# A hybrid encoder layer on one core: order of copies and differences, banks of the latent projections, first x block

## Chip, core and metric

The kernel runs on one core of one Trainium2 chip. The metric is the device time of one execution in microseconds (us); the median of three runs before the change is 1478.06 us (1475.95 to 1479.08). TensorE is called PE here, VectorE DVE, ScalarE ACT, GpSimd POOL, and SyncE's DMA queue SP, as in the profile.

## The reference

One encoder layer on 256 tokens of width 2048, all in float32. A projection of the normalised input feeds two groups of eight heads; the stretch that matters below lies where the first group ends and the second begins:

```python
h = rmsnorm(x, ln_mix); proj = h @ w_in
q_na, k_na, v_na, c_q, c_kv, k_rope = split(proj)          # widths 1024 x3, 512, 256, 64
y_na  = neighbourhood_attention(q_na, k_na, v_na, na_rpb)  # 8 heads of 128, softmax with bias
q  = rmsnorm(c_q, q_norm) @ w_uq      # 8 heads: 128 latent + 64 rotary columns
kv = rmsnorm(c_kv, kv_norm) @ w_ukv   # 8 heads: 128 keys + 128 values
y_mla = softmax((q_nope k_nope^T + rope(q_rope) rope(k_rope)^T) * s) v
x = x + concat(rmsnorm(y_na), rmsnorm(y_mla)) @ w_out
x = x + memory_attention(rmsnorm(x), rmsnorm(mem))         # 4 heads, 256 memory tokens
x = x + swiglu(rmsnorm(x));  return rmsnorm(x)
```

## The kernel before

**Two parts of every operand.** Each float32 operand is split into a high part (ACT copies it into the format fp32r) and a low part (DVE subtracts the high part from the source). `split` (L107) issues one copy and one difference. A product is three matmuls: high by high, high by low, low by high (`products`, L220; `products_fm`, L202, with the weights as the stationary side).

**Weights** come as 496 pieces of 128x1024, two to a DMA on SP, through three raw buffers. `Weights.piece` (L158) keeps up to two pieces split ahead of the one in use (one ahead for the first 16), so every piece costs ACT one copy (`whi`, L110) and DVE one difference (`wlo`, L111), in the same queues as all other work. The first piece is split in two halves, and between them `first_x` splits the first two blocks of x (`xs`, L113 and L114).

**PSUM** has two pools. `psm` (L70) has two buffers of two banks for the long accumulations `pm`; `psa` (L71) has four buffers of one bank for everything short: `pt` (a turn, that is four transposes, L295), `ps` (scores), `py` (a head's output), `pv`, `pc`. A buffer is free when its last reader is done.

**Order.** The main program issues the long products in a written order. Side work (turns, scores, softmax, splits of results) sits in generators in `Background` (L167), advanced by `bg.tick()` after each block of products, so that short work lies between long products. Each engine runs its own instructions strictly in the order issued; an instruction whose wait isn't over holds up all behind it.

**The latent stretch** (L605 to L618): `project_v(0)`, `project_k(0)`, `project_v(1)`, `project_k(2)`, the rotary part of q, `project_q(0)`, `project_q(1)`, then the output projection, with `project_q(2)` and `(3)` inside it. Results go to `ml` (values in the first half, keys in the second), `qn` and `rt`. `project_k` (L573) and `linear_fm` (L208, used by `project_q`) take a `psm` buffer per pair of heads, each of its two tiles of 128x256 in a bank of its own. `split_v` (L343) splits a `psm` buffer in two parts, one per half of the tokens. Beside it, the last head of the first group (`s`, `pk`, `py`, `vy_na`, and `sq`, the square of its output) and the normalised q latent (`ct`, turned into `cs` by `turn_job`, L303) are finished.

Of the kernel before, what the change touches and what calls it, by code (L numbers as in the profile page):

```python
# [60 lines left out]
def tile_hybrid_encoder(ctx, tc, x, xt, mem, memt, gains, fgain, rope, rpb, weights, out):  # L61
# [21 lines left out]

    def load_x(j, queue):
        xf[j] = scr.tile([P, 2, T], F32, name="xf", tag=("ev", "gate")[j % 2])
        queue.dma_start(xf[j], x[:, 2 * j:2 * j + 2, :])

    load_x(0, nc.scalar)

# [14 lines left out]
    ready = const.tile([P, TT], F32, name="ready")  # L104
    nc.scalar.activation(ready, neghalf, AF.Copy)

    def split(dst_hi, dst_lo, src, scale=None):  # L107

        if scale is None:
            ordered(nc.scalar.activation(dst_hi, src, AF.Copy))  # L110
            ordered(nc.vector.tensor_sub(dst_lo, src, dst_hi.bitcast(F32)))  # L111
        else:
            ordered(nc.scalar.activation(dst_hi, src, AF.Copy, scale=scale))  # L113
            ordered(nc.vector.scalar_tensor_tensor(dst_lo, src, scale, dst_hi.bitcast(F32),  # L114
                                           op0=OP.mult, op1=OP.subtract))

    class Weights:

# [14 lines left out]
        def split(self):  # L133
            p = self.done
            self.done += 1
            r, j = divmod(p, 2)
            cuts = (0, PE_EL // 2, PE_EL) if p == 0 else (0, PE_EL)
            cuts = [slice(j * PE_EL + a, j * PE_EL + b) for a, b in zip(cuts, cuts[1:])]
            self.load(r + (1 if p < 2 else 1 + j if p < EARLY else RAWS))
            raw = self.raw[r]  # L140
            if p < 2:
                for c in cuts:
                    nc.sync.dma_start(raw[:, c], weights[r, :, c])
                    if c.start == 0:
                        nc.sync.dma_start(gain, gains)
            if p >= N_PIECE - HELD:
                hi, lo = (self.held[:, p - N_PIECE + HELD, i] for i in range(2))
            else:
                hi = wp.tile([P, PE_EL], F32R, name="whi", tag="whi", bufs=SPLITS)
                lo = wp.tile([P, PE_EL], F32R, name="wlo", tag="wlo", bufs=SPLITS)  # L150
            for c in cuts:
                if c.start and p == 0:
                    self.first_x()
                d = slice(c.start - j * PE_EL, c.stop - j * PE_EL)
                split(hi[:, d], lo[:, d], raw[:, c])
            self.parts[p] = hi, lo

        def piece(self):  # L158
# [60 lines left out]

    def products(o, ak, t, hi, lo, first, last):  # L220

# [81 lines left out]
    def turn_job(src, f0, nf, dst, g0=None, wait=2):  # L303

        for f in range(0, nf, 2):
            pt = turn(src, f0 + f)
            if g0 is None:
                d = dst(f, 2)
                split(d[:, :, 0, :], d[:, :, 1, :], pt)
# [32 lines left out]

    def split_v(pm, dst, rc=None):  # L343

        for t in range(TT):
            v = (pm[t] if isinstance(pm, list) else pm[:, t, :]).rearrange("p (h d) -> p h d", d=P)
            ts_ = slice(t * P, (t + 1) * P)
            split(dst[:, :, 0, ts_], dst[:, :, 1, ts_], v, None if rc is None else rc[:, t:t + 1])


    def softmax_steps(s, scale, pkp, done):

        nm = scr.tile([P, TT], F32, name="nm", tag="nm", bufs=4)
# [19 lines left out]
        split(pk[:, :, 0, :], pk[:, :, 1, :], pt)  # L373
        done(pk)

    def mm_values(py, v, pk):
# [10 lines left out]
    with ExitStack() as at:  # L387
# [17 lines left out]
        def split_x(j):  # L405
            for i in range(2):
                k = 2 * j + i
                split(xs[:, k, 0, :], xs[:, k, 1, :], xf[j][:, i, :], gain[:, G_MIX + k:G_MIX + k + 1])

        wt.first_x = lambda: split_x(0)  # L410
        n_x = KB // 2
        for j in range(n_x):
            ks = range(2 * j, 2 * j + 2)
# [49 lines left out]
        def compressed(pm, w, name, b0, nb_):  # L463
# [17 lines left out]
            if name == "kv":  # L481
                kr = scr.tile([P, TT, 2, ROPE], F32, name="kr", tag="kr")
                for t in range(TT):
                    rotate(kr[:, t, 0:1], kt[:, t:t + 1, :], t, 1)
                    nc.gpsimd.tensor_copy(kr[:, t, 1], kr[:, t, 0])
                yield W_TR
                pt = turn(kr.rearrange("p t j c -> p t (j c)"), 0, 1)
                for i in range(2):
                    rows = slice(i * ROPE, (i + 1) * ROPE)
                    split(krs[i][rows, 0, :], krs[i][rows, 1, :], pt[rows, 0, :])  # L490

        bg.add(compressed(linear(xs, KB, cw=KVR), RANK_KV, "kv", 4, 2))

# [5 lines left out]
        def head_out(vy, h, acc, g0, pk):  # L499

            assert done[g0] == h
            done[g0] += 1
            py = psa.tile([P, T], F32, name="py", tag="a")
            mm_values(py, vy[:, h], pk)
            split(vy[:, h, 0, :], vy[:, h, 1, :], py, gain[:, g0 + h:g0 + h + 1])
            square_into(acc, py[:, None, :], h == 0)

        def na_head(h, qt, wait):
            yield wait
            pt = turn(qt, 2 * (h % 2))  # L510
            qk = nap.tile([P, 2, 2, T], F32R, name="qk", tag="qk", bufs=2)
            split(qk[:, :, 0, :], qk[:, :, 1, :], pt)
            yield W_QK
            ps = psa.tile([P, TT, T], F32, name="ps", tag="a")
            for t in range(TT):
# [10 lines left out]
        def rope_job(pm):  # L526
# [5 lines left out]
            for f in range(0, 4, 2):  # L532
                pt = turn(rt, f)
                qr = ap.tile([P, 2, 2, T], F32R, name="qr", tag="qr", bufs=2)
                split(qr[:, :, 0, :], qr[:, :, 1, :], pt)
                qrs[f], qrs[f + 1] = qr[:, 0], qr[:, 1]
                yield 2

# [21 lines left out]
        def q_job(pair, pm):  # L560
            yield 1
            qn = mlp().tile([P, 2, 2, T], F32R, name="qn", tag="qn", bufs=4)
            split(qn[:, :, 0, :], qn[:, :, 1, :], pm)
            qns[pair] = qn

        def k_job(pair, pm):
            yield 1
            kn = kns[:, 2 * pair:2 * pair + 2]
            split(kn[:, :, 0, :], kn[:, :, 1, :], pm)

        def project_q(pair):
            bg.add(q_job(pair, linear_fm(cs, 4)))
# [1 line left out]
        def project_k(pair):  # L574
            hi, lo = wt.piece()
            for i in range(2):
                pm = psm.tile([P, 2, 2 * T], F32, name="pm", tag="pm")
                for k in range(2):
                    for f in range(2):
                        s = slice(k * 512 + i * 256 + f * P, k * 512 + i * 256 + (f + 1) * P)  # L580
                        products_fm(pm[:, f, 0:T], hi[:, s], lo[:, s], cs[:, 4 + k], k == 0, k == 1)
                    bg.tick()
                bg.add(k_job(pair + i, pm[:, :, 0:T]))

        def project_v(i):
            split_v(linear(cs[:, 4:6], 2), vy_ml[:, 4 * i:4 * i + 4])
# [45 lines left out]
    with ExitStack() as at:  # L632
# [5 lines left out]
        def load_mem():  # L638
            for i in range(4):
# [2 lines left out]
                yield 8  # L642
                for j in range(0, 4, 2):
                    yield 8
                    for k in range(4 * i + j, 4 * i + j + 2):
                        split(ms[:, k, 0, :], ms[:, k, 1, :], r[:, k - 4 * i, :], gain[:, G_MEM + k:G_MEM + k + 1])
# [38 lines left out]
        def xv_job(h, pm):  # L685
# [3 lines left out]
            for j in range(4):  # L689
                py = psa.tile([P, T], F32, name="py", tag="a")  # L690
                mm_values(py, vn[:, j], pks[h])
                o = block(os_, 4 * h + j)
                split(o[:, 0, :], o[:, 1, :], py)
                yield 2

        for h in range(XH):
# [171 lines left out]
```

## Time and profile before

| | us |
|---|---|
| median of three runs (lowest, highest) | 1478.06 (1475.95, 1479.08) |
| the profiled execution's own time | 1475.9 |
| its span, first to last instruction | 1474.0 |
| PE busy in the span | 1452.6 |
| DVE busy | 806.5 |
| ACT busy | 701.4 |
| mean granted TensorE clock | 0.997 |

The span and the profiled execution's own time differ by 1.9 us of start and end. Matmuls are pipelined: a row of PE has the time from its start to its modelled end, and the next one starts before that end. So a gap between two matmuls costs the distance of their starts less the usual distance, which is more than the idle time that a row shows.

### The profile page before, as it was taken

To read this page: it belongs to the slowest core of one execution; us is meant where nothing else is said; L and a number is where in the kernel's file an instruction comes from. 1 tells how busy PE (TensorE), PEld (TensorE's weight loads), DVE (VectorE), ACT (ScalarE), POOL (GpSimd) and SP (SyncE) were. 2 spreads that over 40 slices of the span, in tenths; PEclk is the share of its full clock that TensorE was granted. 3 is DMA by queue.
4 is the path that set the end of the run, shared out by engine and by line. 5 is a ranking of instruction groups with operands and counts; after the bars stand their busy time and mean duration, and the time that the engine had idled before them with its cause. 6 is when DMAs were issued, how large, how long until landed. Compare 5 with 4: busy or idle time off the path is not lost.

```text
span 1474.0 us, 17024 instructions
## 1 busy us (share of the span) xinstructions
PE 1452.6 (99%) x6860; PEld 1214.0 (82%) x6860; DVE 806.5 (55%) x908; ACT 701.4 (48%) x934; POOL 22.1 (2%) x39
## 2 busy tenths in 40 slices
PE   9999989999999999999999999999999999999997
PEld 7888878888888888888888888888888888888886
DVE  5576667666545555555555555455454445555554
ACT  5656554456555454445454444444343444444443
POOL 0000000000000000000000000000000000000000
PEclk9999999999999999999999999999999999999999
DMA  9794443355665444545555555555555555555553
GB/s 345 243 246 159 153 142 127 131 212 173 232 232 179 146 169 149 179 162 197 175 196 186 185 198 187 187 197 178 196 200 192 186 194 192 183 197 187 185 199 114
DMA packets 48717, 275.89 MB, mean 187 GB/s; under 512 B 12992, under 2 KB 13120, under 8 KB 16576
## 3 DMA queue, kind: packets, MB, share of 16 engines
q1 hardware_dynamic: 48208, 273.51, 54.6%
q10 hardware_dynamic: 432, 1.31, 0.3%
q8 instruction: 53, 0.87, 0.2%
q14 instruction: 24, 0.20, 0.0%
HBM read 272.71 MB, written 3.05 MB: 187 GB/s over the span
## 4 chain that ended last, share of the span: by engine, by line
PE 95%; DVE 2%; ACT 1%; DMA 1%; issue 1%; POOL 0%; SPq 0%; POOLq 0%; ACTq 0%
PE pm L223 28%; PE pm L225 28%; PE pm L224 28%; PE pt L300 2%; PE ps L195 2%; PE py L195 2%; PE pv L224 1%; PE pv L225 1%; PE pv L223 1%; DVE wlo L111 1%; DMA raw<-in_weights 1%; PE pl L225 0%; PE pl L223 0%; PE pl L224 0%; ACT whi L110 0%
## 5 line engine op out<-in xcount | busy, mean ns | idle before, releaser
L111 DVE TENSOR_TENSOR wlo<-raw,whi 128x1024 fp32r<-128x1024 f32 (+1 forms) x493 | 601.9, 1222 | 539.5 <-ACT whi L110 538.9
L110 ACT ACTIVATE whi<-raw 128x1024 fp32r<-128x1024 f32 (+1 forms) x493 | 520.5, 1058 | 534.6 <-PE pm L225 502.9
L223 PE MATMUL pm<-whi,x3s 128*128 128x512 f32 x704 | 275.8, 392 | 0.0
L225 PE MATMUL pm<-whi,x3s 128*128 128x512 f32 x704 | 274.1, 389 | 0.0
L224 PE MATMUL pm<-wlo,x3s 128*128 128x512 f32 x704 | 273.9, 389 | 0.0
L225 PEld LDWEIGHTS pm<-whi,x3s 128*128 128x128 f32 x704 | 132.1, 188 | 27.7
L224 PEld LDWEIGHTS pm<-wlo,x3s 128*128 128x128 f32 x704 | 132.2, 188 | 26.8
L223 PEld LDWEIGHTS pm<-whi,x3s 128*128 128x128 f32 x704 | 132.2, 188 | 26.8
L223 PE MATMUL pm<-whi,ms 128*128 128x512 f32 x256 | 101.7, 397 | 0.0
L224 PE MATMUL pm<-wlo,ms 128*128 128x512 f32 x256 | 99.9, 390 | 0.0
L225 PE MATMUL pm<-whi,ms 128*128 128x512 f32 x256 | 99.8, 390 | 0.0
L223 PE MATMUL pm<-whi,ha 128*128 128x512 f32 x224 | 87.5, 391 | 0.0
L225 PE MATMUL pm<-whi,ha 128*128 128x512 f32 x224 | 87.2, 389 | 0.0
L224 PE MATMUL pm<-wlo,ha 128*128 128x512 f32 x224 | 87.1, 389 | 0.0
L223 PE MATMUL pm<-whi,xs 128*128 128x512 f32 (+1 forms) x192 | 74.2, 387 | 0.2 <-ACT whi L110 0.2
L224 PE MATMUL pm<-wlo,xs 128*128 128x512 f32 (+1 forms) x192 | 72.4, 377 | 0.8 <-DVE wlo L111 0.8
L225 PE MATMUL pm<-whi,xs 128*128 128x512 f32 (+1 forms) x192 | 72.5, 378 | 0.0
L225 PEld LDWEIGHTS pm<-whi,ms 128*128 128x128 f32 x256 | 48.1, 188 | 10.4
L223 PEld LDWEIGHTS pm<-whi,ms 128*128 128x128 f32 x256 | 48.2, 188 | 8.9
L224 PEld LDWEIGHTS pm<-wlo,ms 128*128 128x128 f32 x256 | 48.2, 188 | 8.7
L223 PE MATMUL pm<-whi,x2s 128*128 128x512 f32 x128 | 50.0, 391 | 0.0
L225 PE MATMUL pm<-whi,x2s 128*128 128x512 f32 x128 | 49.8, 389 | 0.0
(240 smaller groups left out, 1918.3 us busy)
## 6 DMA issues: line engine op xcount, KB each, us to landing
raw<-in_weights SPq DMA_DIRECT2D x247, 1024.0 KB, 5.0
xr<-in_xt SPq DMA_DIRECT2D x2, 1024.0 KB, 11.2
bias<-skew SPq DMA_DIRECT2D x16, 128.0 KB, 8.3
mtok<-in_memt SPq DMA_DIRECT2D x4, 512.0 KB, 5.1
mraw<-in_mem SPq DMA_DIRECT2D x4, 512.0 KB, 5.6
xf<-in_x SPq DMA_DIRECT2D x7, 256.0 KB, 8.4
fg<-in_fgain SPq DMA_DIRECT2D x1, 1024.0 KB, 9.6
out<-xr SPq DMA_DIRECT2D x2, 512.0 KB, 3.8
```

Of the source, the lines that this page charges most:

```text
L110: ordered(nc.scalar.activation(dst_hi, src, AF.Copy))
L111: ordered(nc.vector.tensor_sub(dst_lo, src, dst_hi.bitcast(F32)))
L195: ordered(nc.tensor.matmul(ps, a[:, u, :], b[:, v, :], start=first and i == 0, stop=last and i == 2))
L223: ordered(nc.tensor.matmul(o, ak[:, 0, ts_], hi, start=first, stop=False))
L224: ordered(nc.tensor.matmul(o, ak[:, 0, ts_], lo, start=False, stop=False))
L225: ordered(nc.tensor.matmul(o, ak[:, 1, ts_], hi, start=False, stop=last))
L300: ordered(nc.tensor.transpose(pt[:, f, t * P:(t + 1) * P], src[:, t, (f0 + f) * P:(f0 + f + 1) * P], ident))
```

## The change

Three edits.

1. `split` takes several parts and issues all copies, then all differences. Callers that had a loop over two parts (`split_v`, `turn_job` with a gain, the blocks of x, the memory's blocks) now pass both at once.
2. `linear_fm` and `project_k` take one bank of `psa` per pair of heads (tile `pf`) in place of a `psm` buffer. Both 256-column tiles lie in that bank; the loop over them is now outside the loop over the contraction, so that one tile is finished before the next begins. The ticks stand at the same distances.
3. The first block of x comes in two DMAs of one half each, both issued on ACT's queue. `first_x` splits the first half between the halves of the first weight piece and the second half after it.

```diff
     def load_x(j, queue):
         xf[j] = scr.tile([P, 2, T], F32, name="xf", tag=("ev", "gate")[j % 2])
-        queue.dma_start(xf[j], x[:, 2 * j:2 * j + 2, :])
+        for i in range(2) if j == 0 else (slice(0, 2),):
+            queue.dma_start(xf[j][:, i], x[:, 2 * j:2 * j + 2, :][:, i])
...
-    def split(dst_hi, dst_lo, src, scale=None):
-
-        if scale is None:
-            ordered(nc.scalar.activation(dst_hi, src, AF.Copy))
-            ordered(nc.vector.tensor_sub(dst_lo, src, dst_hi.bitcast(F32)))
+    def split(*parts):
+
+        for hi, lo, src, scale in parts:
+            if scale is None:
+                ordered(nc.scalar.activation(hi, src, AF.Copy))
...
+        for hi, lo, src, scale in parts:
+            if scale is None:
+                ordered(nc.vector.tensor_sub(lo, src, hi.bitcast(F32)))
...
                 if c.start and p == 0:
-                    self.first_x()
+                    self.first_x((0,))
...
+            if p == 0:
+                self.first_x((1,))
...
-        pm = psm.tile([P, 2, 2 * T], F32, name="pm", tag="pm")
-        for k in range(nk):
-            if k % 4 == 0:
-                hi, lo = wt.piece()
-            for f in range(2):
+        pm = psa.tile([P, 2, T], F32, name="pf", tag="a")
+        assert nk == 4
+        hi, lo = wt.piece()
+        for f in range(2):
+            for k in range(nk):
                 s = slice(k % 4 * T + f * P, k % 4 * T + (f + 1) * P)
-                products_fm(pm[:, f, 0:T], hi[:, s], lo[:, s], block(a, k), k == 0, k == nk - 1)
-            bg.tick()
-        return pm[:, :, 0:T]
+                products_fm(pm[:, f, :], hi[:, s], lo[:, s], block(a, k), k == 0, k == nk - 1)
+                if k % 2:
+                    bg.tick()
+        return pm
...
             else:
-                for j in range(2):
-                    d = dst(f + j, 1)
-                    split(d[:, 0, 0, :], d[:, 0, 1, :], pt[:, j, :], gain[:, g0 + f + j:g0 + f + j + 1])
+                d = dst(f, 2)
+                split(*((d[:, j, 0, :], d[:, j, 1, :], pt[:, j, :], gain[:, g0 + f + j:g0 + f + j + 1])
+                        for j in range(2)))
...
+        parts = []
         for t in range(TT):
...
-            split(dst[:, :, 0, ts_], dst[:, :, 1, ts_], v, None if rc is None else rc[:, t:t + 1])
+            parts.append((dst[:, :, 0, ts_], dst[:, :, 1, ts_], v, None if rc is None else rc[:, t:t + 1]))
+        split(*parts)
...
-                pm = psm.tile([P, 2, 2 * T], F32, name="pm", tag="pm")
-                for k in range(2):
-                    for f in range(2):
+                pm = psa.tile([P, 2, T], F32, name="pf", tag="a")
+                for f in range(2):
+                    for k in range(2):
```

What the built programs show: the instructions of each engine stand in the same order as before (but for the loops' inner order and the first x block); what differs is what they wait for. In brackets are the engines or DMA semaphores that a row waits for.

PE, second tile of keys and the last head's output behind it, before: the tile's first matmul waits for a buffer of `psm`.

```order
L204 MATMUL pm<-cs,whi 128x256 [waits DVE_49,PE_49]
L205 MATMUL pm<-cs,whi 128x256
L206 MATMUL pm<-cs,wlo 128x256
...
L195 MATMUL py<-pk,vy_na 128x256 [waits Activation_49]
L195 MATMUL py<-pk,vy_na 128x256 x5
L223 MATMUL pm<-whi,cs 128x512 [waits DVE_49]
```

The same place on PE after the change, down to the turn of the q latent.

```order
L211 MATMUL pf<-cs,whi 128x256 [waits PE_49]
L212 MATMUL pf<-cs,whi 128x256
L213 MATMUL pf<-cs,wlo 128x256
...
L202 MATMUL py<-pk,vy_na 128x256 [waits Activation_49]
L202 MATMUL py<-pk,vy_na 128x256 [waits DVE_49]
L202 MATMUL py<-pk,vy_na 128x256 x4
L231 MATMUL pm<-whi,cs 128x512
...
L308 MATMUL pt<-ident,ct 128x128 [waits DVE_49,PE_49]
L308 MATMUL pt<-ident,ct 128x128 [waits DVE_49]
```

The keys and the values behind them no longer wait for DVE; the turn does, for `ct`, which it did not have to name before.

ACT, the two copies of the first values (`ml` from `pm`, 4x128) and of the first turned q latent (`cs`), before.

```order
L110 ACTIVATE ml<-pm 128x4x128 [waits PE_49]
L110 ACTIVATE ml<-pm 128x4x128 [waits DVE_49]
L110 ACTIVATE whi<-raw 128x1024
L110 ACTIVATE ml<-pm 128x2x256 [waits PE_49]
...
L113 ACTIVATE cs<-pt,gain 128x256 [waits PE_49]
L113 ACTIVATE cs<-pt,gain 128x256 [waits DVE_49]
```

The same place on ACT after the change.

```order
L112 ACTIVATE ml<-pm 128x4x128 [waits PE_49]
L112 ACTIVATE ml<-pm 128x4x128
L112 ACTIVATE whi<-raw 128x1024
L112 ACTIVATE ml<-pf 128x2x256 [waits PE_49]
...
L114 ACTIVATE cs<-pt,gain 128x256 [waits PE_49]
L114 ACTIVATE cs<-pt,gain 128x256
```

The second copy of a pair waits for nothing of its own; before, it waited for the first difference.

## Rows read from the trace of the kernel before

**Rows 1.** The page, busy us of each engine (share of the span), instructions.

```profile
PE 1452.6 (99%) x6860; PEld 1214.0 (82%) x6860; DVE 806.5 (55%) x908; ACT 701.4 (48%) x934; POOL 22.1 (2%) x39
```

**Rows 2.** Waits of PE, whole span: engine line, releaser, total us, times, longest.

```profile
PE pv L223 <- ACT xs L113: 1.3, 1, 1.3
```

**Rows 3.** Timeline of PE, 200 to 256 us: start, us, what, [idle before, releaser].

```profile
203.95 0.35 PE L204 MATMUL pm<-cs,whi 128*128 128x256 f32 x1 [2.90 <-DVE ml L111]
...
204.26 0.28 PE L206 MATMUL pm<-cs,wlo 128*128 128x256 f32 x1
204.38 0.28 PE L204 MATMUL pm<-cs,whi 128*128 128x256 f32 x1
...
206.73 0.50 PE L223 MATMUL pm<-whi,cs 128*128 128x512 f32 x1 [0.40 <-DVE ml L111]
...
208.22 0.60 PE L300 MATMUL pt<-ident,ct 128*128 128x128 f32 x4
208.58 0.48 PE L223 MATMUL pm<-whi,cs 128*128 128x512 f32 x1
...
212.24 0.36 PE L204 MATMUL pm<-cs,whi 128*128 128x256 f32 x1 [2.02 <-DVE ml L111]
...
217.70 0.50 PE L223 MATMUL pm<-whi,cs 128*128 128x512 f32 x1 [0.38 <-DVE ml L111]
...
226.97 0.35 PE L204 MATMUL pm<-cs,whi 128*128 128x256 f32 x1 [0.66 <-DVE rotb L460]
...
230.56 0.47 PE L223 MATMUL pm<-whi,vy_na 128*128 128x512 f32 x1 [0.49 <-DVE qn L111]
...
255.95 0.47 PE L223 MATMUL pm<-whi,vy_na 128*128 128x512 f32 x1 [1.10 <-DVE qn L111]
```

**Rows 4.** Windows: stretch, its us, busy us of each engine, granted clock, DMA.

```profile
199.47:234.21 34.74, 27.89 (x167) 24.47 (x166) 25.22 (x37) 17.53 (x27) 1.44 (x2) 0.95 0.42 146
212.00:217.00 5.00, 4.76 (x27) 4.79 (x28) 3.54 (x7) 2.98 (x5) 0.00 (x0) 0.66 0.15 21
```

**Rows 5.** Timeline of ACT in the latent stretch.

```profile
200.30 0.60 ACT L110 ACTIVATE ml<-pm 128x512 fp32r<-128x512 f32 x1
202.49 0.60 ACT L110 ACTIVATE ml<-pm 128x512 fp32r<-128x512 f32 x1 [1.59 <-DVE ml L111]
...
207.39 0.38 ACT L255 ACTIVATE sq<-py 128x256 f32<-128x256 f32 x1 [0.55 <-DVE vy_na L114]
207.68 1.05 ACT L110 ACTIVATE whi<-raw 128x1024 fp32r<-128x1024 f32 x1
...
210.41 0.47 ACT L113 ACTIVATE cs<-pt,gain 128x256 fp32r<-128x256 f32 x1 [1.07 <-DVE cs L114]
```

**Rows 6.** Timeline of DVE in the latent stretch.

```profile
201.77 0.68 DVE L111 TENSOR_TENSOR ml<-pm,ml 128x512 fp32r<-128x512 f32 x1
203.12 0.69 DVE L111 TENSOR_TENSOR ml<-pm,ml 128x512 fp32r<-128x512 f32 x1 [0.66 <-ACT ml L110]
204.06 1.23 DVE L111 TENSOR_TENSOR wlo<-raw,whi 128x1024 fp32r<-128x1024 f32 x1 [0.25 <-ACT whi L110]
205.20 0.88 DVE L478 TENSOR_SCALAR ct<-ct,rc_q 128x512 f32<-128x512 f32 x2
205.99 0.68 DVE L111 TENSOR_TENSOR ml<-pm,ml 128x512 fp32r<-128x512 f32 x1
...
209.90 0.48 DVE L114 SCALAR_TENSOR_TENSOR cs<-pt,gain,cs 128x256 fp32r<-128x256 f32 x1
```

**Rows 7.** The chain that ended last, 0 to 16 us: start, us, what.

```profile
3.06 8.47 DMA raw<-in_weights
...
13.93 0.50 PE pv L224
...
14.67 0.23 PE pv L223
```

**Rows 8.** Timeline of SP's queue, 0 to 11 us.

```profile
5.77 0.33 SPq L86 DMA_DIRECT2D xf<-in_x  x1
```

More of the change, by code (lines that the diff above doesn't have):

```diff
@@ L152, in split @@
                 if c.start and p == 0:
-                    self.first_x()
+                    self.first_x((0,))
                 d = slice(c.start - j * PE_EL, c.stop - j * PE_EL)
-                split(hi[:, d], lo[:, d], raw[:, c])
+                split((hi[:, d], lo[:, d], raw[:, c], None))
+            if p == 0:
+                self.first_x((1,))
             self.parts[p] = hi, lo
@@ L308, in turn_job @@
                 d = dst(f, 2)
-                split(d[:, :, 0, :], d[:, :, 1, :], pt)
+                split((d[:, :, 0, :], d[:, :, 1, :], pt, None))
             else:
-                for j in range(2):
-                    d = dst(f + j, 1)
-                    split(d[:, 0, 0, :], d[:, 0, 1, :], pt[:, j, :], gain[:, g0 + f + j:g0 + f + j + 1])
+                d = dst(f, 2)
+                split(*((d[:, j, 0, :], d[:, j, 1, :], pt[:, j, :], gain[:, g0 + f + j:g0 + f + j + 1])
+                        for j in range(2)))
             if f + 2 < nf:
@@ L372, in softmax_steps @@
         pk = pkp.tile([P, TT, 2, T], F32R, name="pk", tag="pk")
-        split(pk[:, :, 0, :], pk[:, :, 1, :], pt)
+        split((pk[:, :, 0, :], pk[:, :, 1, :], pt, None))
         done(pk)
@@ L403, in tile_hybrid_encoder, with split_x @@
         px = parts_tile("x")
[L405 to L410, printed above, removed]
+        def split_x(j, blocks=range(2)):
+            split(*((xs[:, 2 * j + i, 0, :], xs[:, 2 * j + i, 1, :], xf[j][:, i, :],
+                     gain[:, G_MIX + 2 * j + i:G_MIX + 2 * j + i + 1]) for i in blocks))
+        wt.first_x = lambda blocks: split_x(0, blocks)
         n_x = KB // 2
@@ L489, in compressed @@
                     rows = slice(i * ROPE, (i + 1) * ROPE)
-                    split(krs[i][rows, 0, :], krs[i][rows, 1, :], pt[rows, 0, :])
+                    split((krs[i][rows, 0, :], krs[i][rows, 1, :], pt[rows, 0, :], None))
         bg.add(compressed(linear(xs, KB, cw=KVR), RANK_KV, "kv", 4, 2))
@@ L504, in head_out @@
             mm_values(py, vy[:, h], pk)
-            split(vy[:, h, 0, :], vy[:, h, 1, :], py, gain[:, g0 + h:g0 + h + 1])
+            split((vy[:, h, 0, :], vy[:, h, 1, :], py, gain[:, g0 + h:g0 + h + 1]))
             square_into(acc, py[:, None, :], h == 0)
@@ L511, in na_head @@
             qk = nap.tile([P, 2, 2, T], F32R, name="qk", tag="qk", bufs=2)
-            split(qk[:, :, 0, :], qk[:, :, 1, :], pt)
+            split((qk[:, :, 0, :], qk[:, :, 1, :], pt, None))
             yield W_QK
@@ L534, in rope_job @@
                 qr = ap.tile([P, 2, 2, T], F32R, name="qr", tag="qr", bufs=2)
-                split(qr[:, :, 0, :], qr[:, :, 1, :], pt)
+                split((qr[:, :, 0, :], qr[:, :, 1, :], pt, None))
                 qrs[f], qrs[f + 1] = qr[:, 0], qr[:, 1]
@@ L562, in q_job @@
             qn = mlp().tile([P, 2, 2, T], F32R, name="qn", tag="qn", bufs=4)
-            split(qn[:, :, 0, :], qn[:, :, 1, :], pm)
+            split((qn[:, :, 0, :], qn[:, :, 1, :], pm, None))
             qns[pair] = qn
@@ L568, in k_job @@
             kn = kns[:, 2 * pair:2 * pair + 2]
-            split(kn[:, :, 0, :], kn[:, :, 1, :], pm)
+            split((kn[:, :, 0, :], kn[:, :, 1, :], pm, None))
         def project_q(pair):
@@ L576, in project_k @@
             for i in range(2):
-                pm = psm.tile([P, 2, 2 * T], F32, name="pm", tag="pm")
-                for k in range(2):
-                    for f in range(2):
+                pm = psa.tile([P, 2, T], F32, name="pf", tag="a")
+                for f in range(2):
+                    for k in range(2):
                         s = slice(k * 512 + i * 256 + f * P, k * 512 + i * 256 + (f + 1) * P)
-                        products_fm(pm[:, f, 0:T], hi[:, s], lo[:, s], cs[:, 4 + k], k == 0, k == 1)
+                        products_fm(pm[:, f, :], hi[:, s], lo[:, s], cs[:, 4 + k], k == 0, k == 1)
                     bg.tick()
-                bg.add(k_job(pair + i, pm[:, :, 0:T]))
+                bg.add(k_job(pair + i, pm))
         def project_v(i):
@@ L644, in load_mem @@
                     yield 8
-                    for k in range(4 * i + j, 4 * i + j + 2):
-                        split(ms[:, k, 0, :], ms[:, k, 1, :], r[:, k - 4 * i, :], gain[:, G_MEM + k:G_MEM + k + 1])
+                    split(*((ms[:, k, 0, :], ms[:, k, 1, :], r[:, k - 4 * i, :], gain[:, G_MEM + k:G_MEM + k + 1])
+                            for k in range(4 * i + j, 4 * i + j + 2)))
             for g in range(DM // CW):
@@ L692, in xv_job @@
                 o = block(os_, 4 * h + j)
-                split(o[:, 0, :], o[:, 1, :], py)
+                split((o[:, 0, :], o[:, 1, :], py, None))
                 yield 2
```

9 lines of the change are left out of this document (5 added, 4 removed).

## The prediction

> **What bounds the kernel now.** I read the page first: PE is busy 99% of the span [rows 1], 1452.6 of 1474.0 us, so no edit on another engine is worth anything unless it ends a wait of PE, and all of PE's waits together can give some 20 us. Then the list of PE's waits, and the timeline at each: apart from the start [rows 2] and some 1.3 us around 55 and 80 us that the change hardly touches, PE waits at seven places, all between 200 and 256 us [rows 3]. From 256 us to the last products it waits for nothing. Each of the seven is the first matmul of a new accumulation in `psm`, whose two buffers still hold results that DVE has to read: values `ml` before the second keys tile, keys before the second values, and so on to `qn`.
>
> What a gap costs is the distance of two starts. Two 256-column matmuls start 0.12 us apart and each shows 0.28 [rows 3], so a gap costs its idle time plus 0.16. The seven: 2.90 + 0.40 + 2.02 + 0.38 + 0.66 + 0.49 + 1.10 = 7.95, plus 7 x 0.16 = 1.12, gives 9.07 us.
>
> The clock comes on top. Between 212 and 217 us the mean granted clock was 0.66 [rows 4]; of the levels 1.2 and 2.4 GHz that is the lower one for 0.34/0.5 of 5 us, 3.4 us, and half of that, 1.7 us, is lost. The gaps of 2.9, 0.4 and 2.0 us stand just ahead of it. It is the only such stretch: the span's mean is 0.997. The Trainium skill ("TensorE: Matmul & The Clock Gate", HAM oscillation) has the clock fall after idle time between bursts of matmuls; by that rule the 1.7 us go with the gaps, and the trace agrees, since the drop follows the densest group of gaps and no other.
>
> So the most to be had is 9.07 + 1.7 = 10.8 us.
>
> **Banks for latent keys and q.** Eight tiles (four keys, four q) leave `psm`, and only the values, the rotary part and the output projection remain there. Matmuls, their sizes and their number stay; the loop order inside a tile costs nothing, since twelve matmuls in a row on one tile are what six in a row on a `py` tile are today. The seven waits go. What is late next I walk through with durations of rows; instructions of ACT and DVE follow each other about 0.09 before the shown end [rows 6].
>
> PE: from 199.47 the two keys tiles, 24 x 0.12 = 2.88, to 202.35; the last head's output, 6 x 0.12, to 203.07; half of the second values, 6 x 0.23 [rows 7], to 204.45. Then the turn of `ct`. DVE: the first `ml` difference at 201.77 [rows 6]; the second now right behind it at 202.37 in place of 203.12, since ACT made its copy at 200.90 and not at 202.49 [rows 5]; `wlo` (1.23) at 202.97, its copy being done by 202.5, the two `ct` scalings (0.88) at 204.11, done at 204.99. PE starts 0.14 after the DVE result it waits for (203.12 + 0.69 to 203.95), so at 205.13: **a new wait of 0.68.**
>
> Turn (0.36 [rows 3]) to 205.49, second half of the values to 206.87, half of the third keys tile to 207.59, turn to 207.95, other half to 208.67. The fourth keys tile takes the bank of the first turn, and waits for its two `cs` differences. ACT has the square `sq` ahead of them in its queue, which waits for DVE's `vy_na` difference; on DVE that follows `ct` and the keys difference (0.68), so it runs from 205.49 to 205.97. Then `sq` (0.38) from 206.00, `whi` (1.05) to 207.35 [rows 5], two `cs` copies (0.47 each) to 208.1; on DVE `wlo` from 207.38 and two `cs` differences (0.48 each) from 208.52 to 209.39. PE at 209.53: **a new wait of 0.86.**
>
> In the heads' stretch I take 0.3 more, an estimate: a turn of head probabilities there gets the bank of the previous head's output, which ACT reads last, in `sq`, behind a DVE difference. Sum of new waits 0.68 + 0.86 + 0.3 = 1.8. Bounds: 0, and 8 tiles times the longest present wait of 3.1, 25 us. I stay near the walk, which is made of rows of this place.
>
> **Copies first.** On the path it gives the 0.75 us above at `ml` and, at the turned q latent, 1.07 us in which ACT waited between its two copies [rows 5]; the walk contains both. At the other pairs (the later residual turns, the memory's blocks, the cross-attention values) I cost it at nothing: PE waits for none of their results, since weight pieces are split up to two ahead; without that cover each would be worth about what ACT waits at such a pair, 1 us. It can't cost more than the first difference starting one copy later, 0.5 to 0.6 per pair.
>
> A rule speaks against this edit. By the Trainium skill ("PSUM — Partial Sum Buffer", PSUM bank collisions raise a hardware error) no two engines may be in one bank at once, so copies and differences of one bank stay in series in either order, and the bank is free at nearly the same time. By it the first `ml` pair would end at 203.05 in place of 203.81, 0.76 earlier: the sum would be little more than that from this edit alone. Walk and rule agree; so the gain has to come from the banks.
>
> **First x block.** PE waited 1.3 us for the first `xs` [rows 2]. It gives nothing, I think: at 13.93 PE starts at once behind a chain that began with a DMA of weights landing at 11.53 [rows 7], and what came in earlier ahead of that only waits longer there. Bounds: a gain of 1.3. A loss: the extra DMA moves the reuse of semaphores, so that the second full pair of weight pieces is issued on SP only when the first half of x has landed, near where the block after x was issued before, 5.77 [rows 8], some 2 us later. The queue was still full until 11.53, so I take 0.
>
> **Sum.** 9.07 + 1.7 - 1.8 = 9.0 us, so 1475.9 - 9.0 = 1466.9 for an execution like the profiled one. That one lies 2.2 below the median of the runs, 1478.06; the median would be 1478.06 - 9.0 = 1469.1. I forecast **1469 us**.
>
> **Rivals.**
>
> *DVE becomes the bound.* In the 34.74 us from 199.47 DVE is busy 25.22 [rows 4], and the stretch is to shrink by 8.0 us (the six gaps in it, 7.81, and the clock's 1.7, less the two new waits, 1.54), to 26.8. DVE would then be 94% busy, with no slack for handovers from ACT. If each of its 37 instructions lost 0.1 us more, 3.7 of the gain go: 9.0 - 3.7 = 5.3, a median of 1473. For it: today DVE is idle 9.5 us there. Against: most of that idle time is the gaps' own.
>
> *The clock stays as it is.* New waits of 1.5 us remain between 204 and 210; if the clock falls there as before, or falls for another reason, the gain is 7.3: 1471.
>
> *The waits only move.* Pool `psa` has four buffers, and turns, scores and outputs of two heads turn in them. If each of the eight tiles, or the short tile that comes behind it, waits 1.2 us, about the present mean of 9.07/7, 9.6 of the 10.8 go, and the time stays at 1477. Against it: the built order names, for the two keys tiles, no reader that is not long done.
>
> *Slower, from the same pool.* A `ps` bank is held from its scores to both exponentials, and the next tiles queue behind it. From 1.7 us per tile on (13.7 in all) the kernel is slower by over 0.2%; at 2.0 us it is 16 - 10.8 = 5 slower, 1483. Place: 234 to 260 us, with two q tiles among the heads. It needs more than twice the waits of my walk at every tile, where the order shows waits on DVE or ACT for only some of them.
>
> **Chances.** Forecast, 1466 to 1471: 0.70. DVE the bound, 1471 to 1475: 0.14. Clock unchanged, 1470 to 1472: 0.07. Waits moved, 1475 to 1480: 0.06. Slower: 0.03. A difference under 0.2%, 3 us, can't be told from none here. Faster 0.91, within 0.2% 0.06, slower 0.03. The range 1465 to 1474 takes in the first three, less the edges, and the start's bound of 1.3 below. The runs before lie 3.1 us apart, which is in it.
>
> **What would show it.** Right: no wait of PE on `ml` or `qn` in the list of waits; waits of about 0.7 at the first turn of `ct` and 0.9 at the fourth keys tile; a granted clock of 1.00 from 212 to 217; PE at the first output projection near 222.5 in place of 230.56; the copies of a pair back to back on ACT; the chain at 13.93 as before. Wrong: waits of `pf`, `ps` or `py` over 1 us between 234 and 260, weights late after 15 us, or a clock under 1 in a new place.

## The result, and the profile after

The changed kernel takes 1466.36 us (median of 4 runs, 1466.03 to 1467.24) where before takes 1477.12 (4 runs). The ratio is 0.9927, 95% interval 0.9910 to 0.9944: 10.8 us faster. Run again beside later experiments it took 1466.05 (5 runs) against 1477.48 (15 runs), ratio 0.9924 (0.9912 to 0.9937). The forecast of 1469.0 was 2.6 us too high, inside its range of 1465 to 1474. From one profiled execution to the other the span went from 1474.0 to 1464.2 us, 9.8 us, where the sum had 9.0. Line numbers shift: the keys' and q's matmuls are L211 to L213 now, the turn L308, the splits L112 to L119.

The page's line of busy times, to be read beside [rows 1]:

```profile
PE 1451.0 (99%) x6860; PEld 1213.2 (83%) x6860; DVE 803.9 (55%) x908; ACT 698.7 (48%) x934; POOL 22.1 (2%) x39
```

The list of PE's waits (us in total, times, the longest), the whole of it:

```profile
PE idle L392 <- DVE neghalf L94: 1.0, 1, 1.0
PE pm L232 <- DVE wlo L117: 0.8, 1, 0.8
PE pv L232 <- DVE wlo L117: 0.8, 2, 0.5
PE pf L211 <- DVE cs L119: 0.7, 1, 0.7
PE pv L231 <- ACT xs L114: 0.3, 1, 0.3
PE pm L231 <- ACT whi L112: 0.2, 1, 0.2
```

No wait on `ml`, `qn` or `rotb` is left: all seven gaps of [rows 3] are gone. Two small waits stand in their place, at the turn of `ct` and at the fourth keys tile, and a third at a turn of head probabilities. The first and the third are not in the list: a row's modelled end hides them, and the starts show them. PE's timeline, from the first keys tile to the fourth, and the first output projection:

```profile
199.05 0.28 PE L211 MATMUL pf<-cs,whi 128*128 128x256 f32 x1
...
203.79 0.39 PE L233 MATMUL pm<-whi,cs 128*128 128x512 f32 x1
204.30 0.85 PE L308 MATMUL pt<-ident,ct 128*128 128x128 f32 x4
204.91 0.48 PE L231 MATMUL pm<-whi,cs 128*128 128x512 f32 x1
...
208.12 0.28 PE L213 MATMUL pf<-cs,wlo 128*128 128x256 f32 x1
209.10 0.36 PE L211 MATMUL pf<-cs,whi 128*128 128x256 f32 x1 [0.69 <-DVE cs L119]
...
221.82 0.40 PE L231 MATMUL pm<-whi,vy_na 128*128 128x512 f32 x1
```

The turn of `ct` could have started 0.23 behind 203.79, at 204.02, and started at 204.30; it took 0.61 to the next matmul, where it takes 0.36 undisturbed [rows 3]: 0.53 lost. The fourth keys tile could have started at 208.24 and started at 209.10: 0.86 lost. The first output projection stands at 221.82, where before had it at 230.56 [rows 3].

The third wait is in the heads' stretch, ACT's row first, then PE's:

```profile
243.77 0.38 ACT L260 ACTIVATE acc_ml<-py 128x256 f32<-128x256 f32 x1 [0.55 <-DVE ml L119]
243.87 0.28 PE L213 MATMUL pf<-cs,wlo 128*128 128x256 f32 x1
244.21 0.66 PE L308 MATMUL pt<-ident,pr 128*128 128x128 f32 x4
244.62 0.36 PE L211 MATMUL pf<-cs,whi 128*128 128x256 f32 x1
```

The turn could have started at 243.99 and started at 244.21, behind the square of the previous head's output (done at 244.15), which had waited 0.55 for DVE. It took 0.41 in place of 0.36: 0.27 lost.

Two stretches (us, busy us of PE, PEld, DVE, ACT, POOL, granted clock, DMA), the second to be read beside [rows 4]:

```profile
199.47:225.00 25.53, 24.71 (x160) 21.98 (x160) 23.71 (x36) 16.36 (x27) 1.44 (x2) 1.00 0.48 166
212.00:217.00 5.00, 5.00 (x27) 4.30 (x26) 4.85 (x8) 2.50 (x4) 0.00 (x0) 1.00 0.62 210
```

The clock is at its upper level throughout both, and DVE is busy 23.71 of 25.53 us, 93%.

Copies and differences now lie in pairs. ACT, then DVE, against [rows 5] and [rows 6]:

```profile
199.87 1.09 ACT L112 ACTIVATE ml<-pm 128x512 fp32r<-128x512 f32 x2
...
205.57 0.39 ACT L263 ACTIVATE sq<-py 128x256 f32<-128x256 f32 x1 [2.26 <-DVE vy_na L119]
...
206.80 0.83 ACT L114 ACTIVATE cs<-pt,gain 128x256 fp32r<-128x256 f32 x2
```

```profile
201.34 1.28 DVE L117 TENSOR_TENSOR ml<-pm,ml 128x512 fp32r<-128x512 f32 x2
202.54 1.21 DVE L117 TENSOR_TENSOR wlo<-raw,whi 128x1024 fp32r<-128x1024 f32 x1
203.67 0.88 DVE L487 TENSOR_SCALAR ct<-ct,rc_q 128x512 f32<-128x512 f32 x2
```

At the start PE meets the weights of the chain at 13.77, where it was 13.93 [rows 7].

### The profile page after: what moved, and what is told of

It is laid out like the page before. It is cut to its first block, busy times and chain, and to the rows that moved or that the text cites. A ratio compares the mean times of both kernels' runs of the same rounds, so it can differ in the third digit from the quotient of the medians.

```text
span 1464.2 us, 17034 instructions
## 1 busy us (share of the span) xinstructions
PE 1451.0 (99%) x6860; PEld 1213.2 (83%) x6860; DVE 803.9 (55%) x908; ACT 698.7 (48%) x934; POOL 22.1 (2%) x39
## 4 chain that ended last, share of the span: by engine, by line
PE 97%; DVE 1%; DMA 1%; issue 0%; ACT 0%; POOL 0%; SPq 0%; POOLq 0%; ACTq 0%
PE pm L231 29%; PE pm L233 29%; PE pm L232 29%; PE pt L308 3%; PE ps L202 2%; PE py L202 2%; PE pv L232 1%; PE pv L233 1%; PE pv L231 1%; DMA raw<-in_weights 1%; PE pl L232 0%; PE pl L231 0%; PE pl L233 0%; PE pf L211 0%; PE pf L213 0%
## 5 line engine op out<-in xcount | busy, mean ns | idle before, releaser
L112 ACT ACTIVATE whi<-raw 128x1024 fp32r<-128x1024 f32 (+1 forms) x493 | 521.3, 1059 | 539.7 <-PE pm L233 515.8
```

What stands on the lines that cost most here:

```text
L112: ordered(nc.scalar.activation(hi, src, AF.Copy))
```

## The experiments

Eleven runs follow, the last of them the changed kernel once more. Each is the kernel named with the edit shown. Where spans are compared, they are those of single, profiled executions. The start alone makes these differ: PE's wait near 55 us ends at 54.95 in the execution of before and at 56.57 in another with the same code up to there. "Start taken out" means that this difference is subtracted. Medians still contain it.

**Banks alone.** Edit 2 in the kernel before; the order of the splits and the x block as they were.

```
-        pm = psm.tile([P, 2, 2 * T], F32, name="pm", tag="pm")
+        pm = psa.tile([P, 2, T], F32, name="pf", tag="a")
```

> Before with the latent keys and q in single banks of psa, and nothing else of the change. My theory: the banks carry most of the gain, and copies first adds the 0.75 us at the ml pair and the 1.07 us at the turned q latent, so this kernel is about 9.9 - 1.8 = 8.1 us faster than before (ratio near 0.9945), with no wait of PE on ml or qn, a granted clock of 1.00 from 212 to 217 us, and longer waits at the first turn of ct (about 1.2) and at the fourth keys tile (about 1.9). Rival, order doesn't matter (copies and differences of one bank stay in series either way): 9.7 to 9.9 us faster, ratio 0.9934, waits as after. Rival, the pair order is what frees PE: under 5 us faster.

Measured: 1470.17 against 1477.92, ratio 0.9940 (0.9927 to 0.9954), 7.8 us faster. PE's waits from 200 us on:

```profile
206.36 0.85 PE L301 MATMUL pt<-ident,ct 128*128 128x128 f32 x4 [1.23 <-DVE ct L479]
211.79 0.36 PE L204 MATMUL pf<-cs,whi 128*128 128x256 f32 x1 [1.35 <-DVE cs L114]
219.43 0.38 PE L206 MATMUL pf<-cs,wlo 128*128 128x256 f32 x1 [0.26 <-DVE wlo L111]
226.27 0.50 PE L225 MATMUL pm<-wlo,vy_na 128*128 128x512 f32 x1 [0.85 <-DVE wlo L111]
```

No wait on `ml` or `qn`: the banks take all seven gaps away by themselves. The first two waits are those of the changed kernel, and by the starts of rows they cost 1.1 and 0.7 us more; the last two the changed kernel doesn't have. They come from ACT standing between the two copies of a pair, at four pairs in this stretch; two of them:

```profile
203.01 0.60 ACT L110 ACTIVATE ml<-pm 128x512 fp32r<-128x512 f32 x1 [1.58 <-DVE ml L111]
...
210.65 0.47 ACT L113 ACTIVATE cs<-pt,gain 128x256 fp32r<-128x256 f32 x1 [1.32 <-DVE cs L114]
```

What ACT loses there its weight copies (`whi`) lose too, then DVE's `wlo` behind them, and at 226.27 PE waits for one. So copies first is worth about 3.7 us on top of the banks, by the spans (1468.6 less 1464.2) with the start (0.68) taken out. The medians, which hold the x block and the start as well, give 3.0 to 4.1: gains over before of 10.8 or 11.4 less 7.8, or 1470.17 less 1466.05. The rival that order doesn't matter falls, and with it the prediction's sentence that the gain has to come from the banks.

**Copies first alone.** Edit 1 in the kernel before.

```
-            ordered(nc.scalar.activation(dst_hi, src, AF.Copy))
-            ordered(nc.vector.tensor_sub(dst_lo, src, dst_hi.bitcast(F32)))
+        for hi, lo, src, scale in parts:
...
+                ordered(nc.scalar.activation(hi, src, AF.Copy))
...
+        for hi, lo, src, scale in parts:
...
+                ordered(nc.vector.tensor_sub(lo, src, hi.bitcast(F32)))
```

> Before with copies first in every split of several parts, keys and q still in psm, first x block in one transfer. My theory: the gap of 2.90 us at the second keys tile and that of 2.02 us at the third shrink by some 0.7 each, the clock still falls near 212 us, and the kernel is 1 to 2 us faster (ratio 0.9987 to 0.9993). Rival, copies first alone carries a large part: 4 us or more, with the gaps on ml gone. Rival, it delays the first difference of each pair: slower by some 0.5 us at each of the two gaps, ratio 1.0005 or more.

Measured: 1473.69 against 1477.92, ratio 0.9964 (0.9951 to 0.9978), 4.2 us faster, at least twice what I expected. Two of the gaps on `ml` remain, and the two of 0.4 us are gone:

```profile
203.82 0.55 PE L208 MATMUL pm<-cs,whi 128*128 128x256 f32 x1 [2.14 <-DVE ml L116]
212.83 0.36 PE L208 MATMUL pm<-cs,whi 128*128 128x256 f32 x1 [1.98 <-DVE ml L116]
```

The profiled execution was the slowest of the five, and the clock fell twice in it (0.50 from 204 to 206 us and from 214 to 216). Its span of 1473.9 is no shorter than that of before, so the gain is shown by the medians. The next run's profile also has two falls, in what is before's code from 60 us on; beside that one it is 2.7 us shorter with the start taken out. The wait of PE on `kr` near 79 us (0.3 before) is gone as well; the kernels without copies first all have it. The banks (7.8) and the copies (4.2) alone make 12.0, together with the x block 11.4: nearly additive.

**First x block alone.** Edit 3 in the kernel before.

```
-        queue.dma_start(xf[j], x[:, 2 * j:2 * j + 2, :])
+        for i in range(2) if j == 0 else (slice(0, 2),):
+            queue.dma_start(xf[j][:, i], x[:, 2 * j:2 * j + 2, :][:, i])
```

> Before with the first x block in two transfers and nothing else. My theory: PE's wait for the first xs falls from 1.26 to some 0.3 us, but PE meets the weights that landed at 11.53 us again, and only 0.1 to 0.2 us are left behind 13.9 us: ratio 0.9999, not to be told from 1. Rival: the saved 0.9 us go through to the end, ratio 0.9994.

Measured: 1477.40 (12 runs) against 1477.92, ratio 0.9996 (0.9986 to 1.0006): not to be told from 1. PE's first wait fell from 1.3 to 0.3 us, and PE met the weights again at 14 us. This run is worth more for something else. From 60 us on it is the kernel before, and its profiled execution went another way there. Granted clock is the column ahead of the last two; first a stretch of before, whose 212 to 217 us stand in [rows 4] (0.66), then this one:

```profile
204.00:208.00 4.00, 3.60 (x24) 3.17 (x25) 3.10 (x5) 1.60 (x5) 0.08 (x1) 1.00 0.42 113
```

```profile
204.00:208.00 4.00, 3.84 (x19) 3.88 (x20) 2.63 (x5) 0.72 (x2) 0.00 (x0) 0.57 0.39 92
212.00:217.00 5.00, 3.04 (x17) 3.08 (x18) 3.54 (x6) 3.36 (x6) 0.00 (x0) 0.78 0.00 0
217.00:222.00 5.00, 4.61 (x24) 3.97 (x23) 3.64 (x6) 2.52 (x4) 0.00 (x0) 0.88 0.70 210
```

Here the clock fell twice, the first time right behind the gap of 2.90 us. PE's timeline of it:

```profile
204.16 0.36 PE L207 MATMUL pm<-cs,whi 128*128 128x256 f32 x1 [2.90 <-DVE ml L112]
213.96 0.36 PE L207 MATMUL pm<-cs,whi 128*128 128x256 f32 x1 [2.69 <-DVE ml L112]
219.42 0.50 PE L226 MATMUL pm<-whi,cs 128*128 128x512 f32 x1 [0.39 <-DVE ml L112]
```

From the second keys tile to the third it is 9.80 us, in the profile of before 212.24 - 203.95 = 8.29 [rows 3]: the early fall costs 1.5. From the third keys tile to the rotary part it is 5.46 in both (217.70 - 212.24, and 219.42 - 213.96). With the start taken out the whole span is 1.7 longer than that of before.

**Keys in banks, q as before.** Edit 2 in `project_k` alone.

```
-                pm = psm.tile([P, 2, 2 * T], F32, name="pm", tag="pm")
+                pm = psa.tile([P, 2, T], F32, name="pf", tag="a")
```

> Before with the four latent keys tiles in single banks of psa; the four q tiles stay in psm, the splits keep their order, x is in one transfer. The gaps of 2.90, 0.40, 2.02 and 0.38 us go (with 0.16 each, 6.3 us), those at the q tiles and at the output projection (0.66, 0.49, 1.10) stay. If the clock's fall at 212 us hangs on the gaps just ahead of it, it goes too: 6.3 + 1.7 less waits at ct and cs of up to 3 us, so 5 to 7 us faster (ratio 0.9953 to 0.9966), granted clock 1.00 from 200 to 217. If the clock falls at this time for another reason, it is under 0.8 there again and the gain is 3.3 to 5.3 us.

Measured: 1474.12 against 1477.92, ratio 0.9967 (0.9954 to 0.9979), 3.8 us faster. In the profiled execution the clock was at its upper level, so the fall hangs on the keys' gaps, yet the gain is that of the other case. (Two of its five executions show a mean clock of 0.997, so a fall may be left in those.) The waits at `ct` and `cs` are those of banks alone (1.21 and 1.34), and one more grew:

```profile
200.00:222.00 22.00, 19.10 (x121) 16.55 (x119) 17.30 (x26) 12.92 (x23) 1.44 (x2) 1.00 0.38 132
...
224.12 0.36 PE L204 MATMUL pm<-cs,whi 128*128 128x256 f32 x1 [2.18 <-DVE rotb L460]
```

The wait was 0.66 in before [rows 3]. PE was ready for it 4.4 us earlier than in before (221.9 against 226.3), DVE's result only 2.9. A gap that goes leaves part of itself at the next buffer that still turns on the slower engine.

**Two gaps filled.** Before, with matmuls nobody reads ahead of the second and the third keys tile.

```
+                n = {1: 20, 2: 14}.get(pair + i, 0)
+                for m in range(n):
+                    ordered(nc.tensor.matmul(fill[:, 0, :], hi[:, 0:P], cs[:, 4, 0, :], start=m == 0, stop=m == n - 1))
```

> Before, with matmuls whose result nobody reads put into two of its gaps: 20 of 256 columns (20 x 0.12 = 2.4 us) ahead of the second latent keys tile, where PE was idle 2.90 us, and 14 (1.7 us) ahead of the third, where it was idle 2.02. Every wait on DVE stays. If the clock falls because PE is idle there, it is 1.00 from 200 to 222 us now, the tiles still start when DVE lets them, and the kernel is faster by what the clock took: 1.7 us against the profiled run of before, about 3 us in the median, since its slower runs show a lower mean clock (0.995 at 1479.9 to 1483.0, 0.997 at 1475.9 to 1477.5), with its runs within 1.5 us of each other. If the clock falls for another reason, under 1.00 again and the same time as before or, with the filling late for its place, up to 1 us slower.

Measured: 1477.61 (11 runs, 1475.73 to 1479.84) against 1477.59, ratio 1.0000 (0.9990 to 1.0009): no gain. The profile has the clock at 1.00 from 190 to 262 us, and yet:

```profile
205.26 0.36 PE L204 MATMUL pm<-cs,whi 128*128 128x256 f32 x1 [0.47 <-DVE ml L111]
...
213.57 0.35 PE L204 MATMUL pm<-cs,whi 128*128 128x256 f32 x1 [0.39 <-DVE ml L111]
219.03 0.50 PE L223 MATMUL pm<-whi,cs 128*128 128x512 f32 x1 [1.84 <-DVE ml L111]
```

From the third keys tile to the rotary part it is 5.46 us once more, now at the full clock: the 1.5 us that the clock no longer took are in the wait, 1.84 in place of 0.38 [rows 3]. DVE sets that distance. In the profiled execution of before the low clock was hidden. My expectation of 1.7 to 3 us failed with that. This execution also started late: 56.57 near 55 us, against 54.95. With the start taken out, its span (1475.4) is 0.2 us shorter than that of before.

**Three gaps filled.** The same, with 12 more ahead of the rotary part, where the wait had grown.

```
+        for m in range(12):
+            ordered(nc.tensor.matmul(fill[:, 0, :], cs[:, 4, 0, 0:P], cs[:, 4, 0, :], start=m == 0, stop=m == 11))
```

> Before with unread matmuls in three gaps: 20 and 14 as in the run with two, and 12 more (1.4 us) ahead of the rotary part, where with the two the wait had grown from 0.38 to 1.84 us. The starts of the tiles are set by DVE as in that run, so the profile should show the same distance from the third keys tile to the rotary part (5.46 us), clock 1.00. If the executions of before and of the run with two gaps filled lie 4 us apart because the clock falls at the gaps left, this one's lie within 2 us, near the fastest of before, 1475.9. If the filling is worth nothing in the median, 1477.6 again.

Measured: 1475.93 (11 runs, 1475.09 to 1476.30) against 1477.48 (15 runs, 1475.86 to 1479.31), ratio 0.9988 (0.9979 to 0.9997). The distance is 5.46 again, and no wait above 0.5 us stands between 200 and 222:

```profile
212.63 0.36 PE L204 MATMUL pm<-cs,whi 128*128 128x256 f32 x1 [0.35 <-DVE ml L111]
218.09 0.50 PE L223 MATMUL pm<-whi,cs 128*128 128x512 f32 x1 [0.41 <-DVE ml L111]
```

The executions lie 1.2 us apart in place of 3.5, at mean clocks of 0.998 and 0.999, where those of before show 0.996 and 0.997. The median is 1.55 us lower. Against the profiled execution of before nothing is gained: with the start taken out the spans are equal within 0.1 us. The 1.55 us come from before's other executions, and their clocks fit an early fall as in the x block's profile. Over all 47 executions of before run beside the experiments, the median span is 1474.4 us at a mean clock of 0.997 (one fall in the profiled one), 1476.0 at 0.996 (the x block's profile with its two falls has 0.996) and 1478.3 at 0.995.

That the clock makes all of the spread is not shown. The executions with two gaps filled lie 4.1 us apart, and the fastest and the slowest both show 0.998; eight of the eleven, the median one among them, show no lower clock than with three gaps filled, yet their median is 1.7 us higher. The starts of the two profiled executions differ by 1.25 us (56.57 against 55.32). How much of the 1.55 us is the clock and how much the start stays open.

**Gaps made elsewhere.** The changed kernel, with PE made to wait for a chain of DVE operations in the feed-forward part, once alone and later three times.

```
+                for n, ks in ((20, range(0, 2)), (2, range(2, 6)), (14, range(6, KB))):
+                    gap(n)
+                    linear(x3s, KB, pu, ks)
```

> The changed kernel, with gaps made in the feed-forward part, where it has none: PE waits for a chain of small DVE operations, once alone (about 3 us), and later three times within some 10 us (about 3, 1 and 2 us), like the three gaps of before ahead of its slow stretch. If such gaps are what brings the clock down, it is under 1.00 behind the three, for some 3 us or more, and the time is that of the changed kernel plus the gaps (about 9 to 10 us by their idle time) plus 1.7 or more; behind the single one I expect 1.00, since the gap of 2.90 alone in before was followed by 8 us at full clock. If gaps don't do it, the clock is 1.00 at both and only the gaps' own time is added.

Measured: 1491.05 against 1477.59, 25.0 above the changed kernel. The chains ran longer than meant: gaps of 5.62 us alone, and 5.62, 0.91 and 4.04. Stretches ahead of and behind the single gap (793 to 799), then behind the first and the last of the three:

```profile
780.00:793.00 13.00, 13.00 (x59) 10.77 (x58) 6.13 (x5) 4.98 (x5) 0.00 (x0) 1.00 0.48 163
799.00:801.00 2.00, 2.00 (x6) 1.61 (x7) 1.05 (x1) 0.00 (x0) 0.00 (x0) 0.50 0.03 8
803.00:805.00 2.00, 2.00 (x10) 1.65 (x9) 0.26 (x1) 1.06 (x1) 0.00 (x0) 1.00 0.00 0
940.00:944.00 4.00, 3.97 (x10) 3.20 (x11) 1.11 (x1) 0.00 (x0) 0.00 (x0) 0.50 0.00 0
958.00:962.00 4.00, 4.00 (x11) 3.13 (x10) 0.00 (x0) 0.00 (x0) 0.00 (x0) 0.50 0.74 256
```

Gaps bring the clock down in a place that never had it down, and work brings it back. My expectation for the single gap was wrong, but it was of 5.62 us, not 3. Of the 25.0 us the gaps' idle time is 16.2. Most of the other 8.8 is matmuls at half speed: PE worked some 14.8 us at the lower level (799.1 to 802.3, 940.0 to 945.6, 956.7 to 962.7), and half of that, 7.4, is paid in full, since nothing else is late there.

**The square ahead of the difference.** The changed kernel; in its profile ACT stood 2.26 us at `sq` (above). `mid` is called between the copy and the difference.

```
-            split((vy[:, h, 0, :], vy[:, h, 1, :], py, gain[:, g0 + h:g0 + h + 1]))
-            square_into(acc, py[:, None, :], h == 0)
+            split((vy[:, h, 0, :], vy[:, h, 1, :], py, gain[:, g0 + h:g0 + h + 1]),
+                  mid=lambda: square_into(acc, py[:, None, :], h == 0))
```

> The changed kernel, with the square of each head's output (ACT) put between that output's copy (ACT) and its difference (DVE). In the changed kernel ACT stood 2.26 us at the square ahead of 205.57, because it came behind a DVE difference that had two weights and the ct scalings before it. My theory: the square now runs near 203.2, the next weight copy and the two cs copies come about 1.8 us earlier, and PE's wait of 0.69 at the fourth latent keys tile goes: 0.85 us faster than the changed kernel, 1465.5. Rival: DVE, 93% busy there, ends as late as before whatever ACT does, and the wait stays: 1466.4. Rival: the difference, now behind the square, holds up the output projection: slower by 0.4 or more.

Measured: 1465.83 (4 runs, 1465.29 to 1466.82), where the changed kernel took 1466.05 and 1466.36, too close to tell apart. With the start taken out the span is 0.7 us shorter. The wait on `cs` is gone, but that on `ct` grew; its row in the list of PE's waits:

```profile
PE pt L310 <- DVE ct L489: 0.5, 1, 0.5
```

**Both scalings on ACT as well.**

```
-                ordered(nc.vector.tensor_scalar_mul(ct[:, t, 0:w], ct[:, t, 0:w], r[:, t:t + 1]))
+                ordered(nc.scalar.activation(ct[:, t, 0:w], ct[:, t, 0:w], AF.Copy, scale=r[:, t:t + 1]))
```

> The same, with the two scalings of the compressed rows (0.88 us on DVE) given to ACT. If DVE is what PE waits for from 203 to 209 us, this ends the wait of 0.3 (0.5 with the slow start of the turn) at the first turn of ct as well: 0.5 us below the run with the square moved alone, about 1465.0. Rival: ACT's longer copy (0.62 for one, 1.09 for two) delays the weight copies behind it and a new wait on a copy comes: the same or slower than with the square alone.

Measured: 1465.77 (4 runs), no better. No wait is left from 200 us on, but a new one of 0.71 on `kr` stands at 79.88, where the compressed keys are scaled: the rival, at another tile.

**The scalings on ACT for q alone.** The compressed keys' go back to DVE.

```
+                if name == "q":
+                    ordered(nc.scalar.activation(ct[:, t, 0:w], ct[:, t, 0:w], AF.Copy, scale=r[:, t:t + 1]))
+                else:
+                    ordered(nc.vector.tensor_scalar_mul(ct[:, t, 0:w], ct[:, t, 0:w], r[:, t:t + 1]))
```

> The changed kernel with the square before the difference, and with the two scalings on ACT for the latent q alone; those of the compressed keys stay on DVE, since on ACT they left a new wait of 0.71 us on kr at 79.88. My theory: from 60 us on no wait of PE of 0.2 us or more is left, neither at kr nor at ct nor at cs, which gives 0.69 + 0.16 and 0.28 + 0.25 less than the changed kernel, 1.4 us: a median near 1465.0, a span of about 1462.8 with an equal start. Rival: DVE and ACT hand the wait to another tile, and the median stays at 1465.8.

Measured: 1464.69 (4 runs, 1464.31 to 1466.32) against 1477.48, ratio 0.9916 (0.9903 to 0.9930). PE's waits, the whole list:

```profile
PE idle L394 <- DVE neghalf L94: 1.0, 1, 1.0
PE pv L233 <- ACT xs L114: 0.9, 1, 0.9
PE pm L234 <- DVE wlo L119: 0.8, 1, 0.8
PE pv L234 <- DVE wlo L119: 0.4, 1, 0.4
PE pm L233 <- ACT whi L112: 0.2, 1, 0.2
```

All stand ahead of 57 us. Its median is 1.4 below that of the changed kernel beside it, as the sum had it, but the runs overlap. The profiles show it better: with the start taken out the span is 1.5 us shorter than that of the changed kernel (1462.7 against 1464.2). It is the best version here.

**The changed kernel again.**

> The changed kernel itself once more, beside the others, to see how far its executions lie apart. If the spread of before comes from its gaps, these lie within 2 us, what the start alone makes (the first weights land up to 1.6 us later in one execution than in another), with a median near 1466.4.

Measured: 1466.05, 1465.43 to 1466.83. With the wait of 0.71 on `cs` as its longest between 60 us and the end, its executions lie 1.4 us apart.

## Why the prediction was right, point by point

- *The seven gaps, 9.07.* Right: all gone, and by the banks alone.
- *The clock, 1.7.* As a part of the sum right, at 1.5 (1.84 less 0.38 with two gaps filled): the clock is 1.00 there, and PE's lost time of both kinds went. As a cost of its own, wrong for the execution it was read from: by the two fillings DVE's `ml` sets that distance at either clock. The rule of the Trainium skill ("TensorE: Matmul & The Clock Gate", HAM oscillation) that the clock falls after idle time between bursts is borne out by the gaps made elsewhere (0.50 behind a gap of 5.62 us).
- *The new wait at `ct`, 0.68.* It was 0.53, at the place named. *At `cs`, 0.86.* It was 0.86.
- *The heads' stretch, 0.3 estimated.* It was 0.27, by the mechanism named: the turn at 244.21 waits for ACT's square of the previous head's output, which waits for a DVE difference.
- *First x block, 0.* PE's wait near 55 us ends 0.16 earlier than before in the profile of the changed kernel and 0.18 later in that of the x block alone: not to be told from the start's own variation.
- *Not counted:* the wait on `kr` near 79 us, worth 0.26, which copies first ended.
- *Not counted either:* the matmul behind a gap takes 0.07 to 0.11 us longer to the next start than usual (203.95 to 204.26 for two, where two take 0.24 [rows 3]). Over the seven gaps that is 0.57 by the rows; behind the new wait at `cs` it is 0.08.
- *The sum.* 9.07 + 0.57 + 1.46 - 0.53 - 0.86 - 0.08 - 0.27 + 0.16 + 0.26 = 9.78; the spans differ by 9.8. Against the forecast's 9.0, the clock was put 0.2 too high and so were the new waits, which cancel. What the sum lacked is the matmuls behind the gaps (0.5), the start and `kr` (0.4).
- *Copies first: 0.75 at `ml`, 1.07 at `cs`, nothing elsewhere.* This valuation failed. The walk held the two, so the sum did not suffer, but beside the banks the edit is worth about 3.7. "PE waits for none of their results, since weight pieces are split up to two ahead" looked at the pairs' results and not at the weight copies queued behind them on ACT; 0.26 and 0.85 at `wlo` in banks alone are that, and the waits at `ct` and `cs` are the greater part of the rest (1.1 and 0.7). The rule of the Trainium skill ("PSUM — Partial Sum Buffer", PSUM bank collisions) can't be the whole of why copies and differences took turns: ACT waited the same way between the two halves of the values (1.58 above), and each half, 512 f32 values per partition, fills a bank by the same page (Specifications). Whether the rest is the order in which the tile's readers and writers are kept I have not tried.
- *"the median would be 1478.06 - 9.0".* This step made 1.8 of the 2.6 us by which the forecast was too high; the other 0.8 is the sum, 9.0 against 9.8. It let the 2.2 us by which the profiled execution lay under the median stay, and in the changed kernel the distance is 0.3. With three gaps filled 1.55 us of the median went. An early fall of the clock, which costs 1.5 us in the x block's profile, would explain them, and the clocks of before's executions fit; the share of the start is not separated.
- *Rivals.* DVE the bound: its premise was right (93% busy), its loss of 0.1 us per instruction was not; what DVE still cost is the waits above. Clock unchanged, waits moved and slower: none seen. "Waits moved" was real where only half of the tiles moved (2.18 on `rotb`).

## What to carry to other kernels

A gap on a buffer costs its idle time and a little more (here some 0.24 us by the starts), and may cost the clock behind it; read in several executions whether the slow stretch ends at a wait that comes at the same time anyway. When the runs spread and the profiled one lies near their fastest end, ask whether the spread has the same cause as the gaps to be removed; if so the median gains more than the profile shows. Before two executions are compared, compare where each stands after the start. A wait shorter than the modelled end of the row before it is in no list; look at the distances of starts. And where two engines take turns at the parts of one tile, look at what is queued behind the first engine's second part, not only at who reads the result.

## What the runs showed of the hardware that was not expected

The same stretch of the same program ran with one fall of the clock in one execution (0.66 from 212 to 217 us) and with two in another (0.57 from 204 to 208, 0.78 and 0.88 from 212 to 222), and over its runs the mean clock goes from 0.997 down to 0.995 as the time goes from 1475.8 up to 1483.0 us. A fall was free where the stretch ended at a wait on DVE (5.46 us from tile to tile at either level) and cost 1.5 us where it came earlier. With no gap above 0.5 us from 200 to 222, or with the single one of 0.7, none of 20 runs had a mean below 0.998; nor had any of the 5 runs of banks alone, whose gaps there are 1.23 and 1.35.
